# A sink column in the score tile and one triangle select instead of two: a sliding-window attention stage inside a two-layer trunk on one core

## The chip, the core and the metric

The kernel runs on one core of a Trainium2 chip. The time is the device time of one execution in microseconds (us). Before the change, three runs took 959.68, 959.81 and 960.17 us (median 959.81). The execution that the profiler recorded took 959.31 us; its span from the first to the last instruction is 957.6 us.

## The reference

Two layers, each on a sequence of 512 tokens with 1024 channels. One projection of the normalised input gives the columns of two branches: a gated linear recurrence (8 heads of 128) and a sliding-window attention (16 query heads of 64 channels, 2 key/value heads, window 128, a learned sink per head). Both are gated, joined, projected back, normalised and added to the input. The attention part, cut to what matters:

```python
# per block n of 128 queries: keys of block n-1 and of block n
s = einsum('bnqkgd,bnskd->bnkgqs', qb, kw) * ATT_SCALE
band = (diff >= 0) & (diff < WINDOW)          # diff = query position - key position
s = where(mask, s, NEG_INF)
p = softmax(concatenate([s, sink], axis=-1), axis=-1)[..., :-1]
o = einsum('bnkgqs,bnskd->bnqkgd', p, vw)
```

A query at place t of its block sees keys s <= t of its own block and keys s > t of the block before, so exactly 128 keys; the sink only adds to the softmax's sum (and to its maximum).

## The kernel before, in words

All activations stay in SBUF; weights stream from memory in 136 pieces of 128x512 per layer. Each piece is split into two fp32r parts, whi on ScalarE (L169) and wlo = raw - whi on VectorE (L170; a few on GpSimd), and every projection product is three matmuls (L175 to L177).

`step()` issues one such triple and lets the conversions of later pieces run ahead. `merge()` interleaves a branch's own stream with the projection of the slabs that come next. The list ORDER sets the order of slabs: keys and values, queries (QA), recurrence inputs (IV), FQ, and so on. After the last query slab, `run()` merges the attention stream with all the projection up to and including the slab FQ. The order of instructions on each engine is then laid down by the compiler's planner, which follows the order in the program where its own times allow; the matmuls in `pin(...)` keep their order among themselves.

The attention stream has 16 steps a layer: 4 groups g of 4 heads by 4 query blocks n. Step i does three things with projection steps between them:

- `att_scores(g, n)`: for n = 0 eight matmuls into one score tile S; for n > 0 eight matmuls of 256 columns (two heads, key blocks n-1 and n) into two tiles S, one after the other. There are three such PSUM tiles (`sc`), taken in turn, and the transposes use them too. VectorE folds the two key blocks into one (L432: where s > t the score of the block before replaces that of the own block), takes the maximum (L433), and makes the exponent's bias from maximum and sink (L436) and the sink's exponent (L438). ScalarE makes four exponents with their sums (L442) and that of the sink (L445). VectorE adds it (L446) and inverts the sum (L447). GpSimd scales P (L449).
- `att_transpose`, two steps later: TensorE transposes P (L455), ScalarE and VectorE split the result into two fp32r halves (L267, L268, tile tag `a`, 2 buffers). For n > 0 GpSimd's affine_select makes two masked copies of both halves (L467): `pcur`, the keys s <= t for the own block (tags `b` and `oy` in turn), and `pprev`, the keys s > t for the block before (tag `q`, 4 buffers).
- `att_value`, four steps later: matmuls of the masked copies with the values of their blocks (L481; 2 for n = 0, 4 for n > 0), a copy on ScalarE (L483) and two additions on VectorE (L487).

`kv_evac` (L327 to L366) rotates the keys of a token tile and stores the values as `vst`; `kst` holds the transposed keys by block. After the attention, `hgrn` begins with a reciprocal per head into a tile of tag `a` (L551). Query tiles of FQ and the rotation tables use tag `q` too.

Of the kernel before, what the change touches and what calls it, by code (L numbers as in the profile page):

```python
# [10 lines left out]
F32 = mybir.dt.float32  # L11
# [54 lines left out]
def hybrid_kernel(ctx: ExitStack, tc: tile.TileContext, x, wkv, win, wout, g_pre, g_post, lbp, ghead, sinks,  # L66
# [28 lines left out]
    def tmp(tag, dt=F32, n=1):  # L95

        t = tp.tile([P, n, 512] if n > 1 else [P, 512], dt, tag=tag, name=tag, bufs=TB[tag])
        return t
# [225 lines left out]
    def layer(l, last):  # L324
        hops = lambda k, tt: tuple(t[:, k, tt * P:(tt + 1) * P] for t in hT[l])

        kst, vst, rot, oa = [], [], [], []  # L327

        def kv_evac(tt, o):
# [24 lines left out]
            def rest():  # L354
                kt = sc()
                ts_ = slice(tt * P, (tt + 1) * P)
# [49 lines left out]
        def att_scores(g, n):  # L406
# [6 lines left out]
            if n == 0:  # L413
                S = sc()
                for h in range(4):
                    for p in range(2):
                        pin(nc.tensor.matmul(S[:, h * P:(h + 1) * P], lhsT=q[:, h, t_], rhs=kst[v][p][:, 0:P],
# [5 lines left out]
            else:  # L423
                for hp_ in range(2):
                    S = sc()
                    for h in range(2):
                        for p in range(2):
                            pin(nc.tensor.matmul(S[:, h * 256:(h + 1) * 256], lhsT=q[:, 2 * hp_ + h, t_],  # L428
                                             rhs=kst[v][p][:, (n - 1) * P:(n + 1) * P],
                                             start=(h == 0 and p == 0), stop=(h == 1 and p == 1)))  # L430
                    Sv = S.rearrange("p (h s) -> p h s", h=2)
                    nc.vector.copy_predicated(Sv[:, :, P:2 * P], am2, Sv[:, :, 0:P])  # L432
                    nc.vector.tensor_reduce(mx_[:, 2 * hp_:2 * hp_ + 2], Sv[:, :, P:2 * P], axis=AX.X, op=ALU.max)  # L433
                    cur += [Sv[:, h, P:2 * P] for h in range(2)]
            negm = sm.tile([P, 4], F32, tag="negm", name="negm")
            nc.vector.scalar_tensor_tensor(negm, mx_, -SCALE, nsnk[:, l, hs], op0=ALU.mult, op1=ALU.min)  # L436
            ds_ = sm.tile([P, 4], F32, tag="ds", name="ds")
            nc.vector.tensor_tensor(ds_, snk[:, l, hs], negm, op=ALU.add)  # L438
            pt = tmp("s")
            sums = sm.tile([P, 4], F32, tag="sums", name="sums")  # L440
            for h in range(4):
                nc.scalar.activation(pt[:, h * P:(h + 1) * P], cur[h], AF.Exp, bias=negm[:, h:h + 1], scale=SCALE,  # L442
                                     accum_out=sums[:, h:h + 1])
# [4 lines left out]
            pv = pt.rearrange("p (h s) -> p h s", h=4)  # L448
# [3 lines left out]
        def att_transpose(g, n, pt, odd):  # L452
# [3 lines left out]
            tt_ = tmp("a", F32R, 2)  # L456
            split_psum(tt_[:, 0], tt_[:, 1], T)
            if n == 0:
                return [(n, tt_[:, 0]), (n, tt_[:, 1])]
            terms = []  # L460
            for which in range(2):
                if which == 0:
# [446 lines left out]
```

## Time and profile before

| | |
|---|---|
| median of three runs | 959.81 us |
| the profiled execution, its span | 959.31 us, 957.6 us |
| busy: TensorE, VectorE, ScalarE, GpSimd | 921.2, 683.7, 478.4, 268.9 us |
| attention stage of layer 0, of layer 1 (read from the trace) | about 79 to 192 us, 551 to 664 us |
| steps with n > 0 | 12 a layer |

PE stands for TensorE's matmuls, DVE for VectorE, ACT for ScalarE, POOL for GpSimd. Busy times of PE contain the filling of its pipeline. "Idle before" is time in which the engine had nothing to run, with the instruction that ended the wait. A line with x2 or more is several instructions of one kind in a row, with the time from the first's start to the last's end.

### The profile page before, as it was taken

How to read it: one execution, taken by the hardware profiler on the slowest of the kernel's cores; microseconds unless marked ns; L12 is line 12 of the kernel's file. 1: busy time of each engine (PE TensorE's matmuls, PEld its weight loads, DVE VectorE, ACT ScalarE, POOL GpSimd, SP SyncE). 2: the span in 40 equal slices, each digit the busy share in tenths (PEclk: the TensorE clock that was granted, in tenths of full speed). 3: DMA queues.
4: the chain of work that ended last, by engine and by line, in shares of the span. 5: the costliest groups of instructions: out<-in, count | busy, mean ns of one | idle time of the engine just before them, and what ended most of it. 6: DMA issues, size and time to landing. Idle time of an engine off the chain costs nothing.

```text
span 957.6 us, 19092 instructions
## 1 busy us (share of the span) xinstructions
PE 921.2 (96%) x7228; PEld 757.5 (79%) x7228; DVE 683.7 (71%) x1382; ACT 478.4 (50%) x1135; POOL 268.9 (28%) x282
## 2 busy tenths in 40 slices
PE   7999999999999999999979998999999999999996
PEld 5888777777878888788868886877788887887885
DVE  5766888786757785765794678878867568849546
ACT  5434656836545462334552365676374545514242
POOL 2322454422231221211231234434322213113102
PEclk9999999999999999999989999999999999999998
DMA  6366433122413343324452775112223123513313
GB/s 227 101 197 201 137 81 89 52 71 67 122 46 89 90 132 89 107 71 112 133 163 66 198 209 155 34 56 88 79 58 98 55 79 100 155 51 107 88 45 132
DMA packets 56716, 101.34 MB, mean 106 GB/s; under 512 B 6448, under 2 KB 8880, under 8 KB 56624
## 3 DMA queue, kind: packets, MB, share of 16 engines
q1 hardware_dynamic: 56624, 100.12, 35.1%
q8 instruction: 57, 0.93, 0.4%
q14 instruction: 35, 0.29, 0.1%
HBM read 87.52 MB, written 12.58 MB: 105 GB/s over the span
## 4 chain that ended last, share of the span: by engine, by line
PE 78%; DVE 11%; ACT 6%; issue 2%; POOL 2%; DMA 1%; SPq 0%; DVEq 0%; POOLq 0%; ACTq 0%
PE pj L175 22%; PE pj L177 22%; PE pj L176 21%; DVE wlo L170 3%; PE sc L583 2%; PE sc L428 2%; PE ac L652 1%; ACT s L442 1%; PE ac L655 1%; PE ac L640 1%; DVE oa L487 1%; PE ac L481 1%; DVE q L600 1%; PE sc L455 1%; PE sc L700 1%
## 5 line engine op out<-in xcount | busy, mean ns | idle before, releaser
L169 ACT CAST whi<-raw 128x512 fp32r<-128x512 f32 x256 | 157.2, 621 | 131.2 <-PE pj L177 61.0
L170 DVE TENSOR_TENSOR wlo<-raw,whi 128x512 fp32r<-128x512 f32 x248 | 190.1, 778 | 44.8 <-ACT whi L169 42.4
L175 PE MATMUL pj<-hhi,wlo 128*128 128x512 f32 x512 | 206.0, 402 | 0.0
L177 PE MATMUL pj<-hhi,whi 128*128 128x512 f32 x512 | 200.1, 391 | 0.0
L176 PE MATMUL pj<-hlo,whi 128*128 128x512 f32 x512 | 199.5, 390 | 0.0
L177 PEld LDWEIGHTS pj<-hhi,whi 128*128 128x128 f32 x512 | 96.1, 188 | 21.0
L175 PEld LDWEIGHTS pj<-hhi,wlo 128*128 128x128 f32 x512 | 96.2, 188 | 18.6
L176 PEld LDWEIGHTS pj<-hlo,whi 128*128 128x128 f32 x512 | 96.3, 188 | 18.0
L175 PE MATMUL pj<-whi,ops 128*128 128x512 f32 x256 | 103.8, 406 | 0.0
L175 PE MATMUL pj<-whi,hlo 128*128 128x512 f32 x256 | 103.0, 405 | 0.0
L176 PE MATMUL pj<-wlo,hhi 128*128 128x512 f32 x256 | 102.1, 399 | 0.0
L177 PE MATMUL pj<-whi,hhi 128*128 128x512 f32 x256 | 101.4, 396 | 0.0
L177 PE MATMUL pj<-whi,ops 128*128 128x512 f32 x256 | 100.1, 391 | 0.0
L176 PE MATMUL pj<-wlo,ops 128*128 128x512 f32 x256 | 99.7, 390 | 0.0
L601 POOL TENSOR_TENSOR k<-k,tot 128x256 f32<-128x256 f32 x80 | 66.0, 844 | 109.5 <-PE sc L583 60.5
L600 DVE TENSOR_TENSOR q<-q,tot 128x256 f32<-128x256 f32 x80 | 48.3, 629 | 14.5 <-PE sc L594 7.6
L442 ACT ACTIVATE s<-sc,negm 128x128 f32<-128x128 f32 x128 | 45.6, 370 | 25.7 <-DVE negm L436 25.4
L449 POOL TENSOR_TENSOR s<-s,sums 128x512 f32<-128x512 f32 x32 | 34.4, 1074 | 83.4 <-DVE sums L447 47.9
L177 PEld LDWEIGHTS pj<-whi,hhi 128*128 128x128 f32 x256 | 48.9, 191 | 10.2
L177 PEld LDWEIGHTS pj<-whi,ops 128*128 128x128 f32 x256 | 48.0, 188 | 10.7
L176 PEld LDWEIGHTS pj<-wlo,hhi 128*128 128x128 f32 x256 | 49.2, 192 | 8.4
L175 PEld LDWEIGHTS pj<-whi,hlo 128*128 128x128 f32 x256 | 48.8, 191 | 8.6
(172 smaller groups left out, 1594.8 us busy)
## 6 DMA issues: line engine op xcount, KB each, us to landing
raw<-in_win_dram SPq DMA_DIRECT2D x192, 256.0 KB, 2.7
raw<-in_wout_dram SPq DMA_DIRECT2D x64, 256.0 KB, 2.7
stack<-rot SPq DMA_DIRECT2D x16, 512.0 KB, 4.4
qs<-stack SPq DMA_DIRECT2D x32, 256.0 KB, 5.0
a<-in_x_dram SPq DMA_DIRECT2D x12, 256.0 KB, 2.9
raw<-in_wkv_dram SPq DMA_DIRECT2D x8, 256.0 KB, 4.0
x_mid<-a SPq DMA_DIRECT2D x8, 256.0 KB, 2.1
a<-x_mid SPq DMA_DIRECT2D x8, 256.0 KB, 2.9
```

The lines of the kernel that those rows point to most:

```text
L169: nc.scalar.copy(hi, v)
L170: (nc.gpsimd if i in on_pool and i % 2 else nc.vector).tensor_tensor(lo, v, hi.bitcast(F32), op=ALU.subtract)
L175: nc.tensor.matmul(o, lhsT=sta[1], rhs=mov[0], start=start, stop=False)
L176: nc.tensor.matmul(o, lhsT=sta[0], rhs=mov[1], start=False, stop=False)
L177: nc.tensor.matmul(o, lhsT=sta[0], rhs=mov[0], start=False, stop=stop)
L428: pin(nc.tensor.matmul(S[:, h * 256:(h + 1) * 256], lhsT=q[:, 2 * hp_ + h, t_], rhs=kst[v][p][:, (n - 1) * P:(n + 1) * P], start=(h == 0 a ...
L442: nc.scalar.activation(pt[:, h * P:(h + 1) * P], cur[h], AF.Exp, bias=negm[:, h:h + 1], scale=SCALE, accum_out=sums[:, h:h + 1])
L449: nc.gpsimd.tensor_tensor(pv, pv, sums.unsqueeze(2).broadcast_to([P, 4, P]), op=ALU.mult)
L455: pin(nc.tensor.transpose(T[:, h * P:(h + 1) * P], pt[:, h * P:(h + 1) * P], ident))
L583: pin(nc.tensor.matmul(L[32 * b:32 * b + 32, c:c + 16], lhsT=k[:, o_:o_ + 32], rhs=qv[:, blk:blk + qu, 1, :], start=True, stop=True, tile_ ...
L600: nc.vector.tensor_tensor(qv[:, :, 1, :], qv[:, :, 1, :], tv[:, :, 0].unsqueeze(2).broadcast_to([P, nb, hh]), op=ALU.mult)
L601: nc.gpsimd.tensor_tensor(kv_[:, :, 0, :], kv_[:, :, 0, :], tv[:, :, 1].unsqueeze(2).broadcast_to([P, nb, hh]), op=ALU.mult)
```

## The change: what it does

For n > 0 the sink becomes one more column of the score tile. The key blocks are stored in falling order (`kst`), so that S holds the own block in columns 0 to 127 and the block before in columns 128 to 255. Key 0 of the block before is never seen; its column 128 is overwritten by the sink divided by the scale (a two-element copy on ScalarE for each S, from the new constant `snk8`). The fold now replaces own columns 1 to 127 where s > t, the maximum and the exponents run over 129 columns, and the sum comes out with the sink in it. The separate sink exponent, its input and its addition remain for n = 0 alone, and the bias becomes a plain multiplication.

For the values, P transposed (both halves, now in a tile of tag `q` for all steps) goes whole to the values of the block before, and one select (s <= t) goes to a stationary of differences, v of the own block minus v of the block before (`vdf`, one buffer of tag `a`, three subtractions with splits a layer in `kv_evac`). Counts of matmuls stay as they are.

```diff
+            kvs[tt] = raw
+            if tt == 1:
+                vdf.append(tmp("a", F32R, 2).rearrange("p v (n c) -> p v n c", n=NT))
+            if tt:
+                dv = sm.tile([P, 2, 64], F32, tag="dv", name="dv", bufs=1)
+                two = lambda r: r[:, 128:256].rearrange("p (v d) -> p v d", v=2)
+                nc.vector.tensor_tensor(dv, two(raw), two(kvs.pop(tt - 1)), op=ALU.subtract)
+                nc.scalar.copy(vdf[0][:, :, tt, 0:64], dv)
+                nc.vector.tensor_tensor(vdf[0][:, :, tt, 64:128], dv, vdf[0][:, :, tt, 0:64].bitcast(F32), op=ALU.subtract)
...
-                    nc.vector.copy_predicated(Sv[:, :, P:2 * P], am2, Sv[:, :, 0:P])
-                    nc.vector.tensor_reduce(mx_[:, 2 * hp_:2 * hp_ + 2], Sv[:, :, P:2 * P], axis=AX.X, op=ALU.max)
-                    cur += [Sv[:, h, P:2 * P] for h in range(2)]
+                    nc.scalar.copy(Sv[:, :, P:P + 1], snk8[:, l, 4 * g + 2 * hp_:4 * g + 2 * hp_ + 2].unsqueeze(2))
+                    nc.vector.copy_predicated(Sv[:, :, 1:P], am2[:, :, 1:P], Sv[:, :, P + 1:2 * P])
+                    nc.vector.tensor_reduce(mx_[:, 2 * hp_:2 * hp_ + 2], Sv[:, :, 0:P + 1], axis=AX.X, op=ALU.max)
+                    cur += [Sv[:, h, 0:P + 1] for h in range(2)]
...
-            nc.vector.scalar_tensor_tensor(negm, mx_, -SCALE, nsnk[:, l, hs], op0=ALU.mult, op1=ALU.min)
-            ds_ = sm.tile([P, 4], F32, tag="ds", name="ds")
-            nc.vector.tensor_tensor(ds_, snk[:, l, hs], negm, op=ALU.add)
-            pt = tmp("s")
+            if n:
+                nc.vector.tensor_scalar(negm, mx_, -SCALE, None, op0=ALU.mult)
...
-            es = sm.tile([P, 4], F32, tag="es", name="es")
-            nc.scalar.activation(es, ds_, AF.Exp)
-            nc.vector.tensor_tensor(sums, sums, es, op=ALU.add)
+            if n == 0:
...
-            tt_ = tmp("a", F32R, 2)
+            tt_ = big.tile([P, 2, 512], F32R, tag="q", name="pall", bufs=QB)
...
-            for which in range(2):
...
+            d = big.tile([P, 2, 512], F32R, tag="oy", name="pcur", bufs=6) if odd else tmp("b", F32R, 2)
+            nc.gpsimd.affine_select(out=d.rearrange("p a (h t) -> p (a h) t", h=4),
...
+            whole, own = terms
+            prods = [(vst[v][:, max(n - 1, 0), :], whole[:, j]) for j in range(2)]
+            if own is not None:
+                prods += [(vdf[0][:, v, n, :], own[:, j]) for j in range(2)]
...
+    snk8 = const.tile([P, DEPTH, ATT_HEADS], F32, name="snk8")
+    nc.vector.tensor_scalar(snk8, snk, 1.0 / SCALE, None, op0=ALU.mult)
```

## Rows read from the trace of the kernel before

**Rows 1.** The page: busy time, share and instructions of each engine; the chain that ended last, by engine.
```profile
PE 921.2 (96%) x7228; PEld 757.5 (79%) x7228; DVE 683.7 (71%) x1382; ACT 478.4 (50%) x1135; POOL 268.9 (28%) x282
...
PE 78%; DVE 11%; ACT 6%; issue 2%; POOL 2%; DMA 1%; SPq 0%; DVEq 0%; POOLq 0%; ACTq 0%
```

**Rows 2.** Busy time of each engine in the attention stages of layer 0 and of layer 1. Columns: stretch, its length, busy us (and instructions) of PE, PE's weight loads, DVE, ACT, POOL, granted clock as a share, DMA share, GB/s.
```profile
79.00:192.00 113.00, 106.26 (x534) 87.08 (x533) 89.01 (x201) 74.79 (x228) 50.09 (x44) 0.97 0.37 108
...
551.00:664.00 113.00, 106.08 (x540) 86.81 (x539) 91.00 (x202) 76.42 (x229) 50.06 (x44) 0.98 0.39 108
```

**Rows 3.** The timeline of PE: the instructions before which it sat idle longest in the two attention stages, and one in layer 1's key/value stage (start us, duration, instruction, idle before it and what ended it).
```profile
105.33 0.84 PE L455 MATMUL sc<-ident,s 128*128 128x128 f32 x4 [1.96 <-DVE negm L436]
...
125.44 1.40 PE L417 MATMUL sc<-kst,qs 128*128 128x128 f32 x8 [1.73 <-ACT s L442]
...
154.69 0.74 PE L428 MATMUL sc<-kst,qs 128*128 128x256 f32 x4 [0.36 <-ACT s L442]
...
161.51 1.43 PE L428 MATMUL sc<-kst,qs 128*128 128x256 f32 x8 [1.27 <-ACT s L442]
...
185.06 0.73 PE L481 MATMUL ac<-pcur,vst 128*128 128x512 f32 x2 [0.56 <-POOL pcur L467]
186.55 0.73 PE L481 MATMUL ac<-pprev,vst 128*128 128x512 f32 x2 [0.30 <-POOL pprev L467]
...
500.99 0.39 PE L175 MATMUL pj<-wkv,hlo 128*128 128x256 f32 x1 [0.94 <-DVE hlo L268]
...
577.90 0.63 PE L455 MATMUL sc<-ident,s 128*128 128x128 f32 x4 [1.95 <-DVE negm L436]
```

**Rows 4.** The timeline of POOL and of DVE ahead of the first three of those gaps.
```profile
98.03 1.10 POOL L467 TENSOR_SCALAR_AFFINE_SELECT pcur<-a 128x1024 fp32r<-128x1024 f32 x1 [0.24 <-DVE negm L436]
99.08 1.54 POOL L467 TENSOR_SCALAR_AFFINE_SELECT pprev<-a 128x1024 fp32r<-128x1024 f32 x1
...
98.21 2.96 DVE L170 TENSOR_TENSOR wlo<-raw,whi 128x512 fp32r<-128x512 f32 x2 [0.18 <-ACT whi L169]
101.09 0.15 DVE L438 TENSOR_TENSOR ds<-snk,negm 128x4 f32<-128x4 f32 x1
...
102.03 0.69 DVE L170 TENSOR_TENSOR wlo<-raw,whi 128x512 fp32r<-128x512 f32 x1
...
119.89 3.92 DVE L170 TENSOR_TENSOR wlo<-raw,whi 128x512 fp32r<-128x512 f32 x3
...
121.73 1.54 POOL L467 TENSOR_SCALAR_AFFINE_SELECT pprev<-a 128x1024 fp32r<-128x1024 f32 x1
...
154.49 1.55 POOL L467 TENSOR_SCALAR_AFFINE_SELECT pprev<-a 128x1024 fp32r<-128x1024 f32 x1
...
153.61 1.47 DVE L170 TENSOR_TENSOR wlo<-raw,whi 128x512 fp32r<-128x512 f32 x1 [0.24 <-ACT whi L169]
155.00 1.04 DVE L446 TENSOR_TENSOR sums<-sums,es 128x4 f32<-128x4 f32 x1
```

**Rows 5.** Groups of instructions by line in layer 0's attention stage (79 to 192 us): count, busy us and mean ns of one, idle time before them and what ended it.
```profile
L170 DVE TENSOR_TENSOR wlo<-raw,whi 128x512 fp32r<-128x512 f32 x25 | 24.4, 994 | 2.3 <-ACT whi L169 1.7
...
L467 POOL TENSOR_SCALAR_AFFINE_SELECT pprev<-a 128x1024 fp32r<-128x1024 f32 x12 | 15.8, 1320 | 0.0
...
L446 DVE TENSOR_TENSOR sums<-sums,es 128x4 f32<-128x4 f32 x16 | 5.1, 318 | 8.2 <-ACT es L445 8.1
...
L445 ACT ACTIVATE es<-ds 128x4 f32<-128x4 f32 x16 | 3.4, 215 | 0.5 <-DVE ds L438 0.5
```

**Rows 6.** Busy time by short stretches around the first gaps (columns as in rows 2; the granted clock is the third number from the end).
```profile
104.00:112.00 8.00, 6.67 (x29) 5.59 (x29) 6.00 (x15) 3.23 (x15) 5.71 (x6) 0.79 0.27 102
120.00:128.00 8.00, 6.27 (x31) 5.21 (x30) 6.64 (x13) 3.59 (x13) 4.31 (x4) 0.88 0.88 228
128.00:136.00 8.00, 8.00 (x39) 6.48 (x38) 6.63 (x15) 4.92 (x20) 5.32 (x5) 0.91 0.01 2
592.00:600.00 8.00, 6.27 (x29) 5.23 (x28) 6.60 (x14) 3.35 (x12) 3.66 (x3) 0.82 0.82 201
```

**Rows 7.** The timeline of one step with n > 0, from its score matmuls to the next step's: PE, DVE, and the first and the last of ACT's four exponents.
```profile
129.59 0.64 PE L428 MATMUL sc<-kst,qs 128*128 128x256 f32 x4
...
132.54 0.43 DVE L432 COPY_PREDICATED sc<-masks,sc 128x256 f32<-128x256 uint8 x1 [0.47 <-PE sc L428]
...
133.93 0.82 DVE L436 SCALAR_TENSOR_TENSOR negm<-mx,nsnk 128x4 f32<-128x4 f32 x1
...
134.83 0.37 ACT L442 ACTIVATE s<-sc,negm 128x128 f32<-128x128 f32 x1
...
135.88 0.37 ACT L442 ACTIVATE s<-sc,negm 128x128 f32<-128x128 f32 x1
...
135.69 0.74 PE L428 MATMUL sc<-kst,qs 128*128 128x256 f32 x4
```

**Rows 8.** A group of the whole span that stands near what the change adds (columns as in rows 5).
```profile
L268 DVE TENSOR_TENSOR kst<-sc,kst 128x128 fp32r<-128x128 f32 x16 | 4.5, 280 | 0.0
```

**Rows 9.** The timeline of DVE in layer 1's key/value stage and at the beginning of layer 0's recurrence, and the busy times of 8 us near the end of layer 0's attention stage (columns as in rows 2).
```profile
502.55 0.68 DVE L170 TENSOR_TENSOR wlo<-raw,whi 128x512 fp32r<-128x512 f32 x1
...
192.18 1.74 DVE L551 RECIPROCAL a<-f 128x256 f32<-128x256 f32 x1
...
168.00:176.00 8.00, 8.00 (x44) 6.72 (x43) 4.04 (x12) 7.89 (x19) 1.72 (x2) 1.00 0.00 0
```

More of the change, by code (lines that the diff above doesn't have):

```diff
@@ L95, in tmp @@
     def tmp(tag, dt=F32, n=1):
-        t = tp.tile([P, n, 512] if n > 1 else [P, 512], dt, tag=tag, name=tag, bufs=TB[tag])
+        t = tp.tile([P, n, 512] if n > 1 else [P, 513] if tag == "s" else [P, 512], dt, tag=tag, name=tag, bufs=TB[tag])
+        t = t[:, 0:512] if tag == "s" else t
         return t
@@ L325, in layer @@
         hops = lambda k, tt: tuple(t[:, k, tt * P:(tt + 1) * P] for t in hT[l])
-        kst, vst, rot, oa = [], [], [], []
+        kst, vst, vdf, rot, oa, kvs = [], [], [], [], [], {}
         def kv_evac(tt, o):
@@ L416, in att_scores @@
                     for p in range(2):
-                        pin(nc.tensor.matmul(S[:, h * P:(h + 1) * P], lhsT=q[:, h, t_], rhs=kst[v][p][:, 0:P],
+                        pin(nc.tensor.matmul(S[:, h * P:(h + 1) * P], lhsT=q[:, h, t_], rhs=kst[v][p][:, (NT - 1) * P:NT * P],
                                          start=(h == 0 and p == 0), stop=(h == 3 and p == 1)))
@@ L440, in att_scores @@
+            pt = tp.tile([P, 513], F32, tag="s", name="pt", bufs=TB["s"])
             sums = sm.tile([P, 4], F32, tag="sums", name="sums")
             for h in range(4):
-                nc.scalar.activation(pt[:, h * P:(h + 1) * P], cur[h], AF.Exp, bias=negm[:, h:h + 1], scale=SCALE,
+                nc.scalar.activation(pt[:, h * P:(h + 1) * P + (n > 0)], cur[h], AF.Exp, bias=negm[:, h:h + 1], scale=SCALE,
                                      accum_out=sums[:, h:h + 1])
-            es = sm.tile([P, 4], F32, tag="es", name="es")
@@ L445, in att_scores @@
-            nc.scalar.activation(es, ds_, AF.Exp)
-            nc.vector.tensor_tensor(sums, sums, es, op=ALU.add)
+            if n == 0:
+                ds_, es = (sm.tile([P, 4], F32, tag=t, name=t) for t in ("ds", "es"))
+                nc.vector.tensor_tensor(ds_, snk[:, l, hs], negm, op=ALU.add)
+                nc.scalar.activation(es, ds_, AF.Exp)
+                nc.vector.tensor_tensor(sums, sums, es, op=ALU.add)
             nc.vector.reciprocal(sums, sums)
-            pv = pt.rearrange("p (h s) -> p h s", h=4)
+            pv = pt[:, 0:512].rearrange("p (h s) -> p h s", h=4)
@@ L455, in att_transpose @@
                 pin(nc.tensor.transpose(T[:, h * P:(h + 1) * P], pt[:, h * P:(h + 1) * P], ident))
[L456 removed]
+            tt_ = big.tile([P, 2, 512], F32R, tag="q", name="pall", bufs=QB)
             split_psum(tt_[:, 0], tt_[:, 1], T)
             if n == 0:
[L459 to L472 removed]
+                return tt_, None
+            d = big.tile([P, 2, 512], F32R, tag="oy", name="pcur", bufs=6) if odd else tmp("b", F32R, 2)
+            nc.gpsimd.affine_select(out=d.rearrange("p a (h t) -> p (a h) t", h=4),
+                                    in_=tt_.bitcast(F32).rearrange("p a (h t) -> p (a h) t", h=4),
+                                    pattern=[[0, 8], [1, P]], compare_op=ALU.is_ge, fill=0.0, base=0, channel_multiplier=-1)
+            return tt_, d
         def att_value(g, n, terms):
@@ L479, in att_value @@
             U = ac()
-            for i, (blk, d) in enumerate(terms):
-                pin(nc.tensor.matmul(U, lhsT=vst[v][:, blk, :], rhs=d, start=(i == 0), stop=(i == len(terms) - 1)))
+            whole, own = terms
+            prods = [(vst[v][:, max(n - 1, 0), :], whole[:, j]) for j in range(2)]
+            if own is not None:
+                prods += [(vdf[0][:, v, n, :], own[:, j]) for j in range(2)]
+            for i, (sta, mov) in enumerate(prods):
+                pin(nc.tensor.matmul(U, lhsT=sta, rhs=mov, start=(i == 0), stop=(i == len(prods) - 1)))
             ul = tmp("u")
```

16 lines of the change are left out of this document (4 added, 12 removed).

## The prediction

> **What bounds the kernel now.** I read the page's busy times and its chain first. PE is busy for 921.2 of 957.6 us, and 78% of the chain that ended last is PE [rows 1]. The change leaves PE's instructions as they are: for n > 0 eight score matmuls of 256 columns, four transposes, four value matmuls, before and after. So it can only win or lose where PE waits, or runs at half its clock.
>
> The second view is the busy time by stage. In the two attention stages PE is idle for 113.00 - 106.26 = 6.7 us and 113.00 - 106.08 = 6.9 us; DVE is busy for 89 and 91 of 113 us, ACT for 75 and 76, POOL for 50 and 50 [rows 2]. No engine but PE is full there, so the question is which wait ends last.
>
> The third is PE's own timeline. Few gaps hold nearly all of that idle time: in layer 0 1.96, 1.73, 0.36 and 1.27 us, where the transposes or scores wait for a PSUM tile that the bias or the exponents of an earlier step still hold, and 0.56 and 0.30 us at the end, where the last value product waits for the two selects [rows 3]. Layer 1 repeats this (its first, 1.95 us, is shown). I take 5.3 us a layer for the first four and 0.86 for the last two.
>
> What made the exponents late? The timeline of DVE and POOL ahead of the gaps shows it: two conversions wlo took 2.96 us together and three took 3.92, while one alone takes 0.69; beside them POOL ran pcur and pprev, which themselves took up to 1.55 us instead of 1.10 [rows 4]. The mean wlo of the stage is 994 ns [rows 5]. A 4-element addition took 1.04 us beside a select [rows 4], its mean being 318 [rows 5]. DVE and POOL hold each other up, the bias of the next step queues behind wlo on DVE, and PE runs dry.
>
> The Trainium skill ("SBUF — State Buffer", section "Who interferes with whom") gives the rule: DVE and POOL share a port pair that one instruction holds to its end, and a DVE instruction contends with a reading GpSimd one if both its inputs lie in SBUF. By it the bias of a step with n > 0, a multiplication with one tensor input after the change, would no longer be held up (it took 0.82 us once); no row here separates the two forms of it, and the sum below doesn't count on it.
>
> Last the clock: it is 0.79 of full in 104 to 112 us, 0.88 and 0.91 in 120 to 136, 0.82 in 592 to 600 [rows 6], each behind a gap of 1.7 us or more; the chip's levels being 2.4 and 1.2 GHz, these are means over stretches at half speed. The time given away is 8 x (0.21 + 0.12 + 0.09 + 0.18) = 4.8 us.
>
> **The change, part by part.**
>
> *Select.* 24 selects go (12 pprev a layer, 15.8 us of POOL busy time in layer 0 [rows 5]). At each gap I take away what the second select cost. Gap 1: 2.96 - 2 x 0.69 = 1.58 us were lost beside selects of 1.10 and 1.54 us; the second's share by length is 0.92, and as the first still delays the pair I take 0.8. Gap 2: 3.92 - 3 x 0.69 = 1.85, half of it 0.9. Gaps 3 and 4: the addition that took 1.04 us disappears, and half of 1.47 - 0.69, 0.4; 1.4 together. The sink's two additions on DVE go as well, some 0.15 us each when nothing holds them up [rows 4]; they stand in the same queue: 0.3 at gaps 1 and 2, 0.2 at gap 4. That is 1.1 + 1.2 + 1.6 = 3.9 of 5.3 us a layer. The bounds: 0, if DVE only waits elsewhere instead, and all 5.3.
>
> *Sink column.* 48 small ACT copies come (two a step), 24 sink exponents of 215 ns go [rows 5]. A 2-element copy isn't in the trace; the nearest row is that exponent, so I take 0.2 us. What matters is the place: the copy has to wait for the S matmuls, and the fold, being written after it and in the same tile, then waits for ACT's queue. Behind the fold on DVE stand the maximum, the bias, and the next wlo; PE waits for these. Before, the fold waited for PE alone [rows 7]. If ACT is free the link costs 0.2; if it has just begun four exponents, 135.88 + 0.37 - 134.83 = 1.4 us and the last reading of the sum more [rows 7], 1.6 in all. ACT is two thirds busy, but much of that can be ordered around the copy, so I take 0.2 + 0.25 for each of the three gaps: 1.35 us a layer against the 3.9, leaving 2.55. From below: nothing, where DVE has other work. From above: 2 x 1.8 at each, which eats the gain twice over.
>
> *Tail.* The products with the whole transposed P need no select, and one select less stands ahead of the last: the second gap goes, the first stays, 0.3 us a layer (0 to 0.86). Against it, ACT is busy for 7.89 of 8 us at 168 to 176 [rows 9]; three steps there bring six copies for three exponents, 6 x 0.2 - 3 x 0.215 = 0.6 us, of which I charge half, 0.3.
>
> *Value differences.* Three times a layer DVE does two operations of 128 columns (the nearest row is 280 ns [rows 8]) and ACT one: 1.7 us of DVE a layer. They are written behind the keys of token tile 1 and later, so behind the last half of the normalised input that PE waits for at 500.99 us [rows 3]. The wlo at 502.55 [rows 9] stands behind the first of them; I charge 0.3 a layer (0 to 0.6). Without that cover it is 1.7 a layer.
>
> *Constant snk8.* One small DVE operation at the start: 0.15 us alone, 1.04 held up by POOL [rows 4]. I take 0.2, nearest to the first.
>
> *Buffers.* `pall` takes one of four `q` tiles for all 16 steps and lives until its value product two steps on: three are live, and one more when the first query tile of FQ comes, where the next split waits for a product that PE did a step before. I charge nothing (0 to 0.5). `vdf` holds one of two `a` tiles until the last value product at 186.55 + 0.73 us; the second reciprocal starts at 192.18 [rows 9], so nothing.
>
> *Clock.* With gaps of about 1.1 us instead of 1.7 to 2.0, the falls should mostly go: the gap of 1.27 us had none behind it, though the one of 1.95 in layer 1 had none either. I take 60% of 4.8: 2.9 (0 to 4.8).
>
> *Sum:* 2 x (2.55 + 0.3) + 2.9 = 8.6 saved; 2 x (0.3 + 0.3) + 0.2 = 1.4 paid; 7.2 us net. The profiled execution took 959.31, so 952.1; the median lies 0.5 above it: 952.6 us.
>
> **Rivals.** About 0.2% (1.9 us) is what a measurement of this kernel can tell from no change.
>
> *All gaps go.* If one select never meets two wlo in a row and the copies fall into ACT's free time, 2 x 6.2 + 4.8 us go and 1.4 are paid: 944. For it: DVE gets rid of some 12 x 0.63 us of small work a layer besides. Against it: the scaling of P, a further POOL operation of 1 us per step, still meets wlo, and all orders change. Chance 0.12.
>
> *The link gives back what the select gave.* The fold waits for ACT about as long as DVE waited for POOL; gaps move, the clock falls as often: 959.8, within 1.9. For it: DVE already waits 8.1 us a layer for ACT's sink exponent [rows 5], and would now wait for two copies a step in its place. Chance 0.17.
>
> *Slower: the link becomes the limit.* In the step shown, S was computed at 129.59 and the next S in the same tile started at 135.69, right when the exponents freed it [rows 7]: 6.1 us of chain in a step of 113 / 16 = 7.06. If each of the two folds waits 1.2 us for ACT, 2.4 are added and perhaps 0.67 (the bias at 0.15, like other small operations, instead of 0.82) saved: the chain is 7.8 us, 0.8 above the step. It decides from 0.95 + 0.67 = 1.6 us a step on. Half of the 24 steps so hit cost 9 us, and the old gaps that remain are paid back by the selects, some 2 to 3: 966. For it: ACT's queue is in order, and copies that the planner puts behind four exponents wait that long. Against: most steps have PE work between to cover it. Chance 0.25.
>
> The Trainium skill ("PSUM — Partial Sum Buffer", section "PSUM bank collisions raise a hardware error") speaks for this rival: two engines must be kept apart by bank, not by address, so the fold has to wait for the copy though their columns differ. No row of before has ACT writing PSUM beside DVE.
>
> My forecast has 0.46. Its own range, from the bounds of the link and of the clock, is 948 to 957. Over all cases I give 944 to 964. Faster by over 0.2%: 0.46 + 0.12 + 0.01 of the second rival = 0.59; same 0.16; slower 0.25.
>
> **What would show it.** Right: POOL's busy time in the stage near 35 us instead of 50; the mean wlo well under 994 ns; PE idle for some 4 us a layer in the stage instead of 6.8; at most one stretch under full clock there; the sink copies at about 0.2 us with short waits of the fold for them. The link is wrong if the fold's waits for ACT sum to over 20 us a layer and PE's gaps end at exponents. The differences are wrong if PE's gap in the key/value stage grows beyond 0.94 + 0.6. The prediction as a whole falls if wlo becomes short and PE's gaps stay: then it wasn't POOL that starved PE.

## The result, and the profile after

The changed kernel took 963.73 us (median of 9 runs, 959.54 to 965.32), the kernel before 959.94 us beside it (9 runs): a ratio of 1.0027, 95% interval 1.0015 to 1.0040. It is slower by 0.27%, where a gain of 7.2 us was forecast. The execution that the profiler recorded took 964.37 us. The nine executions fall into two bunches, three at 959.5 to 960.7 us and six at 963.5 to 965.3; e9 below bears on that.

The page of the changed kernel, the lines that answer to [rows 1]:

```profile
PE 924.9 (96%) x7228; PEld 756.1 (79%) x7228; DVE 667.8 (69%) x1347; ACT 494.8 (51%) x1171; POOL 241.0 (25%) x258
...
PE 66%; DVE 9%; ACT 8%; issue 5%; POOL 2%; DMA 1%; DVEq 0%; POOLq 0%; ACTq 0%
```

DVE and POOL lost work (16 and 28 us), ACT gained 16 us. The first score product comes at 82.90 us instead of 79.18, so the two attention stages are read 4 us later than in [rows 2]; the columns are the same:

```profile
83.00:196.00 113.00, 106.36 (x535) 84.68 (x534) 79.69 (x172) 80.60 (x239) 34.46 (x30) 0.99 0.42 115
555.00:668.00 113.00, 106.83 (x535) 85.21 (x534) 77.82 (x170) 80.65 (x239) 34.39 (x30) 0.98 0.40 113
```

POOL fell from 50 to 34.4 us and the clock rose from 0.97 to 0.99 in layer 0, yet PE still idles 6.6 us there. Where, its timeline says (idle before in brackets, as in [rows 3]):

```profile
95.01 0.96 PE L176 MATMUL pj<-whi,hlo 128*128 128x512 f32 x3 [1.19 <-ACT whi L170]
...
108.22 1.11 PE L427 MATMUL sc<-kst,qs 128*128 128x128 f32 x8 [0.61 <-ACT pt L456]
...
182.99 0.70 PE L494 MATMUL ac<-pall,vst 128*128 128x512 f32 x2 [0.49 <-DVE oa L500]
...
192.93 0.66 PE L471 MATMUL sc<-ident,pt 128*128 128x128 f32 x4 [2.15 <-POOL pt L465]
...
567.68 0.98 PE L176 MATMUL pj<-whi,hlo 128*128 128x512 f32 x3 [1.66 <-ACT whi L170]
```

The gaps of 1.96, 1.73 and 1.27 us are gone. In their place stand two of another kind: a projection that waits for a weight conversion on ACT (95.01; 567.68 is its twin in layer 1), and at the end 2.15 us before the transposes of the last P. The clock falls behind that last one in layer 0 and behind the first one in layer 1; another fall is at the start of the kernel:

```profile
32.00:40.00 8.00, 8.00 (x36) 6.92 (x37) 7.51 (x33) 5.41 (x19) 2.65 (x2) 0.79 0.49 131
...
192.00:200.00 8.00, 7.07 (x26) 5.73 (x27) 7.85 (x13) 5.81 (x11) 3.50 (x4) 0.79 0.25 66
...
568.00:576.00 8.00, 7.54 (x36) 6.10 (x35) 4.68 (x10) 3.96 (x15) 0.52 (x1) 0.79 0.72 243
```

Taking the first score product and the recurrence's first product as milestones: 3.7 us were lost before the first score product (82.90 against 79.18), 0.4 in layer 0's attention (123.70 against 123.34 us, though at the better clock), 1.4 in layer 1's (123.51 against 122.14).

**What made the last P late.** ACT's timeline in the last two steps of layer 0's attention, and POOL's ahead of the last transposes; of ACT only exponents (x1 each) and table loads are copied, of the last step the first and the last exponent:

```profile
166.28 0.38 ACT L456 ACTIVATE pt<-sc,negm 128x129 f32<-128x129 f32 x1
...
166.77 0.37 ACT L456 ACTIVATE pt<-sc,negm 128x129 f32<-128x129 f32 x1
...
167.25 1.28 ACT L539 ACT_TABLE_LOAD   x1
...
169.16 1.28 ACT L456 ACT_TABLE_LOAD   x1
170.45 0.37 ACT L456 ACTIVATE pt<-sc,negm 128x129 f32<-128x129 f32 x1
...
170.93 1.28 ACT L540 ACT_TABLE_LOAD   x1
...
172.84 1.28 ACT L456 ACT_TABLE_LOAD   x1
174.14 0.37 ACT L456 ACTIVATE pt<-sc,negm 128x129 f32<-128x129 f32 x1
...
184.07 0.37 ACT L456 ACTIVATE pt<-sc,negm 128x129 f32<-128x129 f32 x1
...
189.19 0.38 ACT L456 ACTIVATE pt<-sc,negm 128x129 f32<-128x129 f32 x1
...
190.16 1.28 POOL L478 TENSOR_SCALAR_AFFINE_SELECT b<-pall 128x1024 fp32r<-128x1024 f32 x1 [8.69 <-DVE pall L269]
191.41 1.47 POOL L465 TENSOR_TENSOR pt<-pt,sums 128x512 f32<-128x512 f32 x1
```

The last step but one spreads its four exponents over 8.2 us, the last one over 5.5 (184.07 to 189.19 + 0.38), with weight conversions and a gate's activation between them. Before, four lasted 1.4 us, as in [rows 7] (134.83 to 135.88 + 0.37). The scaling of the last P then stood behind a select on POOL that had begun 0.02 us before the inverted sum was there, and PE waited 2.15 us; in layer 1, where the exponents took 4.4 us, it waited 0.98. In the 8.2 us the gates' activations (L539, L540) stand between the exponents, and as these need another function table, each change costs a load of 1.28 us: 28 loads in the span, 22 before. What holds the exponents apart shows in the compiled order of ACT, which names the semaphores that each instruction waits for (Activation_49 is ACT's own):

```
L456 ACTIVATE pt,sums<-sc_79,negm 128x128 [waits DVE_49,PE_49]
L456 ACTIVATE pt,sums<-sc_79,negm 128x128 x3
...
L456 ACTIVATE pt,sums<-sc_80,negm 128x129 [waits DVE_49,Activation_49]
L456 ACTIVATE pt,sums<-sc_80,negm 128x129 [waits Activation_49]
L456 ACTIVATE pt,sums<-sc_78,negm 128x129 [waits Activation_49] x2
```

The heads stand 128 columns apart in `pt`, but an exponent now writes 129. Its last column is the next head's first, so the next exponent must wait until this one's write is done: ACT waits for itself. The 128-column exponents of n = 0 wait for nothing between them.

**And the link**, the fold's wait for the sink copy on ACT. The first step with n > 0 (PE, ACT, DVE, and ACT again: the first exponent and the conversions behind the fourth):

```profile
85.19 1.12 PE L438 MATMUL sc<-kst,qs 128*128 128x256 f32 x8
...
88.97 0.37 ACT L456 ACTIVATE pt<-sc,negm 128x128 f32<-128x128 f32 x1 [2.41 <-DVE negm L451]
...
90.46 0.26 ACT L443 COPY sc<-snk 128x2 f32<-128x2 f32 x2
...
90.69 0.42 DVE L444 COPY_PREDICATED sc<-masks,sc 128x254 f32<-128x254 uint8 x1
...
92.52 0.37 ACT L456 ACTIVATE pt<-sc,negm 128x129 f32<-128x129 f32 x1 [1.80 <-DVE negm L449]
...
94.35 1.65 ACT L170 CAST whi<-raw 128x512 fp32r<-128x512 f32 x3
```

The scores are there at 86.31 us. The copies stand behind the step before's exponents in ACT's queue, and the fold behind the copies: 4.4 us. (Not all of this is the link: in e6 below, without it, the fold of this step still starts 2.6 us after the scores.) The bias and the exponents follow, ACT idling 1.80 us, and behind the exponents the weight conversions for which PE then waits (95.01 above). Over a layer's 24 score tiles the mean from the end of the score product to the start of its fold, worked out from the timelines, is 1.50 us against 0.87 before.

The groups of the stage (79 to 195 us) show the same from the other side:

```profile
L171 DVE TENSOR_TENSOR wlo<-raw,whi 128x512 fp32r<-128x512 f32 x29 | 24.4, 856 | 9.4 <-ACT whi L170 9.1
...
L444 DVE COPY_PREDICATED sc<-masks,sc 128x254 f32<-128x254 uint8 x24 | 9.8, 418 | 2.3 <-ACT sc L443 2.1
...
L443 ACT COPY sc<-snk 128x2 f32<-128x2 f32 x24 | 3.8, 165 | 5.2 <-PE sc L438 5.2
...
L463 DVE RECIPROCAL sums<-sums 128x4 f32<-128x4 f32 x16 | 2.8, 176 | 14.8 <-ACT pt L456 11.0 <-ACT sc L443 3.7
```

DVE's mean wlo fell from 994 ns to 856, a copy takes 165 ns. But DVE now idles for ACT: 9.1 us at wlo, 14.7 at the reciprocal, 2.1 at the fold, where it was 1.7 at wlo and 8.1 at the sum before [rows 5]. Which of these waits cost anything, the experiments have to tell.

### The profile page after: what moved, and what is told of

Same layout as the page of the kernel before. It is cut to its first block, busy times and chain, and to the rows that moved or that the text cites. A ratio compares the mean times of both kernels' runs of the same rounds, so it can differ in the third digit from the quotient of the medians.

```text
span 962.6 us, 19077 instructions
## 1 busy us (share of the span) xinstructions
PE 924.9 (96%) x7228; PEld 756.1 (79%) x7228; DVE 667.8 (69%) x1347; ACT 494.8 (51%) x1171; POOL 241.0 (25%) x258
## 4 chain that ended last, share of the span: by engine, by line
PE 66%; DVE 9%; ACT 8%; issue 5%; POOL 2%; DMA 1%; DVEq 0%; POOLq 0%; ACTq 0%
PE pj L176 18%; PE pj L178 18%; PE pj L177 18%; ACT pt L456 3%; PE sc L596 2%; DVE wlo L171 2%; PE ac L665 1%; PE ac L494 1%; ACT whi L170 1%; PE sc L438 1%; PE ac L668 1%; PE ac L653 1%; PE sc L471 1%; DMA raw<-in_win_dram 1%; POOL pt L465 1%
## 5 line engine op out<-in xcount | busy, mean ns | idle before, releaser
L171 DVE TENSOR_TENSOR wlo<-raw,whi 128x512 fp32r<-128x512 f32 x248 | 184.9, 756 | 51.7 <-ACT whi L170 49.6
L465 POOL TENSOR_TENSOR pt<-pt,sums 128x512 f32<-128x512 f32 x32 | 35.8, 1118 | 109.9 <-DVE sums L463 95.6
L178 PEld LDWEIGHTS pj<-whi,ops 128*128 128x128 f32 x256 | 48.0, 188 | 10.6
L176 PEld LDWEIGHTS pj<-whi,ops 128*128 128x128 f32 x256 | 48.1, 188 | 9.4
```

Of the source, the lines that this page charges most:

```text
L171: (nc.gpsimd if i in on_pool and i % 2 else nc.vector).tensor_tensor(lo, v, hi.bitcast(F32), op=ALU.subtract)
L176: nc.tensor.matmul(o, lhsT=sta[1], rhs=mov[0], start=start, stop=False)
L178: nc.tensor.matmul(o, lhsT=sta[0], rhs=mov[0], start=False, stop=stop)
L465: nc.gpsimd.tensor_tensor(pv, pv, sums.unsqueeze(2).broadcast_to([P, 4, P]), op=ALU.mult)
```

## The experiments

All ratios are against the kernel before on the same chip, with 95% intervals. The main theory: one select less is worth what was forecast, and the sink column takes it back by two separate costs: the exponents put in series because each writes into the next one's place (below, the overlap), and the copy in front of the fold (the link). The rivals are in the texts on record. Four runs came first.

**e1: heads 129 columns apart in P.**

```diff
-            pt = tp.tile([P, 513], F32, tag="s", name="pt", bufs=TB["s"])
+            pt = tp.tile([P, 516], F32, tag="s", name="pt", bufs=TB["s"])
+            W_ = P + (n > 0)
...
-                nc.scalar.activation(pt[:, h * P:(h + 1) * P + (n > 0)], cur[h], AF.Exp, ...
+                nc.scalar.activation(pt[:, h * W_:(h + 1) * W_], cur[h], AF.Exp, ...
```

> The change with one thing altered: the exponents of the four heads are written 129 columns apart instead of 128, so that no head's sink column lies on the next head's first column. Theory A (the overlap makes each exponent wait for the one before, and lets the planner put other work between them): exponents of a step start 0.34 us apart again instead of 0.49, the function-table loads on ACT fall from 28 to 22, the attention stream ends some 10 us earlier than in the changed kernel, PE's waits in the attention stages fall by 3 to 5 us a layer: 955 to 958 us. Theory B (the sink copy in front of the fold is what costs): the time stays within 2 us of the changed kernel's 963.7. Theory C (the loss is all in the start stage): 962 to 964 us.

**e2: the select alone** (the scores, the sink and the order of keys' use as before; the one select and the value differences as changed, with the keys in rising order; diff against the kernel before).

```diff
-            for which in range(2):
...
-                d = big.tile([P, 2, 512], F32R, tag="q", name="pprev", bufs=QB)
...
+            return tt_, d
```

> The kernel before with the select part alone: one select, whole P to the values of the block before, value differences; the sink as it was. Theories A and B: the prediction's term for the selects stands by itself, PE's waits in the attention stages fall by 2 us a layer or more and the clock falls less often: 950 to 956 us. Theory C: the key/value stage of layer 0 costs the same 3 us here, because the value differences cause it: 957 to 961 us.

**e3: without the constant** (the copy scales the sink itself).

```diff
-                    nc.scalar.copy(Sv[:, :, P:P + 1], snk8[...].unsqueeze(2))
+                    nc.scalar.activation(Sv[:, :, P:P + 1], snk[...].unsqueeze(2), AF.Copy, scale=float(1.0 / SCALE))
...
-    nc.vector.tensor_scalar(snk8, snk, 1.0 / SCALE, None, op0=ALU.mult)
```

> The change without its constant snk8: the sink copy multiplies by 8 itself on ACT, one small DVE operation less at the start. Theory C1 (that one operation moves the key rotation of layer 0 behind a DVE operation that GpSimd holds up, 1.94 us of PE idle instead of 0.90, and a fall of the clock behind it): the first score matmul comes at 79 to 81 us instead of 82.9, the time is 960 to 962 us. Rival C2 (the value differences or chance do it): first score matmul at 82 to 83.5, 963 to 965 us.

**e4: the sink column alone** (two selects and the two stationaries of values as before; diff against the changed kernel).

```diff
-            return tt_, d
+            for which in range(2):
...
-                nc.vector.tensor_tensor(dv, two(raw), two(kvs.pop(tt - 1)), op=ALU.subtract)
```

> The kernel before with the sink column alone: 129 columns, sink copies, both selects kept. Theory A: exponents 0.49 us apart, more table loads than before (30 by the order of the program), slower than before by 4 us or more: 964 to 970 us. Theory B: the same time, but with the fold's waits for ACT's copies above 10 us a layer. If neither, it is within 2 us of before.

| | median us | ratio |
|---|---|---|
| e1 | 958.64 | 0.9972 (0.9958 to 0.9986) |
| e2 | 951.13 | 0.9896 (0.9877 to 0.9916) |
| e3 | 961.00 | 1.0004 (0.9990 to 1.0018) |
| e4 | 970.35 | 1.0093 (1.0074 to 1.0113) |

The select alone gives 10 us, the sink column alone costs 9: the sum is 1.1 us under the kernel before, where the changed kernel is 2.6 above it; e9 below finds most of that difference at the start. In e2 the stage shows what the forecast had described, the gaps with their old causes but smaller:

```profile
106.12 0.63 PE L464 MATMUL sc<-ident,s 128*128 128x128 f32 x4 [1.08 <-DVE negm L445]
...
124.07 1.11 PE L426 MATMUL sc<-kst,qs 128*128 128x128 f32 x8 [0.92 <-ACT s L451]
```

They were 1.96 and 1.73 us [rows 3], and no stretch of the stage is under full clock:

```profile
80.00:193.00 113.00, 108.59 (x556) 88.35 (x555) 90.85 (x212) 76.57 (x232) 35.45 (x32) 1.00 0.41 115
```

In e1 the table loads are back at 22 and a block of four exponents at 1.55 us (3.1 in the changed kernel), while the time from scores to fold stays at 1.48: the two costs come apart. The time is 0.6 us above e1's range, and one sign failed: PE's waits were to fall by 3 to 5 us a layer, and fell from 6.6 to 6.0 and from 6.2 to 5.8; the gap at the weight conversion stays (1.15 us in layer 0). e4 ends 0.35 us above its range. e3 is not apart from the kernel before, nor clearly from the changed one; its time lies in the theory's range, but its first score product still comes at 82.61 us, as the rival had it. The constant isn't needed for the late start.

Then the two costs were taken one at a time.

**e5: the sink copy on DVE** (pitch 129).

```diff
-                    nc.scalar.copy(Sv[:, :, P:P + 1], snk8[...].unsqueeze(2))
+                    nc.vector.tensor_copy(Sv[:, :, P:P + 1], snk8[...].unsqueeze(2))
```

> The changed kernel with a pitch of 129 columns a head in pt (as in the run e1, 958.6 us) and the sink copy moved from ScalarE to VectorE, right in front of its fold. Nothing of the computation is changed. Theory 'two costs' (serialised exponents, which the pitch has taken away, and the link through ScalarE): the fold no longer waits for ScalarE, so the time from the last score product to the fold's start falls from 1.5 us towards the 0.9 us of the kernel before; the copy itself stands on VectorE with about 0.17 to 0.25 us, 48 times in a layer's 24 steps, 8 to 12 us a layer of VectorE's time that mostly lies beside other work. I expect 952 to 956 us and the sum of the gaps of TensorE in the two attention stages down from 6 to under 5.5 us a layer. Rival 'any op in front of the fold costs the same, whichever engine holds it': 957 to 960 us, gaps at 6 us. Rival 'VectorE becomes the limit': 960 us and more, with gaps that end at folds whose own wait is VectorE's queue.

**e6: the copy behind the maximum** (pitch 129; fold and maximum over 128 columns, the bias by the minimum with the sink).

```diff
-                    nc.scalar.copy(Sv[:, :, P:P + 1], snk8[...].unsqueeze(2))
...
-                    nc.vector.tensor_reduce(mx_[:, 2 * hp_:2 * hp_ + 2], Sv[:, :, 0:P + 1], axis=AX.X, op=ALU.max)
+                    nc.vector.tensor_reduce(mx_[:, 2 * hp_:2 * hp_ + 2], Sv[:, :, 0:P], axis=AX.X, op=ALU.max)
+                    nc.scalar.copy(Sv[:, :, P:P + 1], snk8[...].unsqueeze(2))
...
+            nc.vector.scalar_tensor_tensor(negm, mx_, -SCALE, nsnk[:, l, hs], op0=ALU.mult, op1=ALU.min)
```

> The changed kernel with a pitch of 129 columns in pt, but fold and maximum run over the 128 key columns alone, ScalarE's sink copy comes behind the maximum, and the bias takes the sink in by the minimum with nsnk as in the kernel before. The exponent still covers 129 columns, so the small ops for the sink's exponent and its addition stay away. The computation is whole. Theory 'link': nothing stands between the score products and the fold any more, the copy waits on ScalarE in front of the exponents that follow it on the same engine anyway: 950 to 954 us, beside the 951.1 us of the select alone (e2), with the time from score products to the fold at 0.9 to 1.0 us. Rival 'the copies themselves cost (48 ScalarE ops a layer, between exponents)': 955 to 959 us.

**e7: the overlap alone** (diff against the changed kernel; maximum and bias as in e6).

```diff
-                    nc.scalar.copy(Sv[:, :, P:P + 1], snk8[...].unsqueeze(2))
...
-            if n == 0:
+            if True:
                 ds_, es = (sm.tile([P, 4], F32, tag=t, name=t) for t in ("ds", "es"))
```

> The one select with value differences (e2, 951.1 us), the keys in the reversed order, and exponents over 129 columns at a pitch of 128, so that each writes one column of the next head's place; no sink copy, the sink is added by the four small ops of the kernel before. Column 128 holds the score of a key outside the window, so the row sums take in one extra score. Theory 'serialised exponents': each exponent starts only once the one before has ended, 0.49 us apart instead of 0.34, other work of ScalarE gets between them, with up to six more table loads of 1.28 us a layer; the block of four lasts about 3 us instead of 1.55, and the time is 954 to 958 us. Rival 'the overlap costs nothing by itself, it was the copy': 951 to 952 us.

**e8: e7 with heads 129 columns apart** (the diff of e1 on top).

> The same as e7 with a pitch of 129 columns a head, so that no two exponents write one column; the extra score stays in the sums. Theory 'serialised exponents': the block of four exponents is back at about 1.55 us, the order on ScalarE that of e2, and the time 950.5 to 952.5 us; the difference from e7 is the price of the overlap alone. Rival 'one column more for each exponent, or the reversed keys, cost': as e7.

| | median us | ratio |
|---|---|---|
| e5 | 954.50 | 0.9934 (0.9917 to 0.9951) |
| e6 | 951.31 | 0.9900 (0.9884 to 0.9915) |
| e7 | 958.01 | 0.9976 (0.9964 to 0.9988) |
| e8 | 950.32 | 0.9899 (0.9883 to 0.9915) |

e7 and e8 differ in nothing but the distance of the heads, and by 0.0077 of 960 us: 7.4 us (each lies within 0.2 us of its range). ACT's exponents in the first step with n > 0, in e7 (its second and third):

```profile
91.10 0.37 ACT L452 ACTIVATE pt<-sc,negm 128x129 f32<-128x129 f32 x1
91.37 0.19 ACT L452 ACTIVATION_READ_ACCUMULATOR pt<-sc,negm 128x1 f32 x1
91.59 0.37 ACT L452 ACTIVATE pt<-sc,negm 128x129 f32<-128x129 f32 x1
```

and in e8:

```profile
88.14 0.37 ACT L453 ACTIVATE pt<-sc,negm 128x129 f32<-128x129 f32 x1 [0.36 <-DVE negm L447]
88.40 0.19 ACT L453 ACTIVATION_READ_ACCUMULATOR pt<-sc,negm 128x1 f32 x1
88.50 0.36 ACT L453 ACTIVATE pt<-sc,negm 128x129 f32<-128x129 f32 x1
...
88.84 0.37 ACT L453 ACTIVATE pt<-sc,negm 128x129 f32<-128x129 f32 x1
```

Each takes 0.37 us in both; they start 0.49 us apart in e7, 0.36 and 0.34 in e8. The 0.14 us make 3 x 0.14 us in 24 steps, 10 us of ACT time, part of it beside other work. More is what gets in between: a block of four lasts 2.79 us in the mean against 1.55, with 26 table loads against 22. How the price divides between the two wasn't measured.

e6 leaves nothing of the copy's cost that the medians show (0.9900 against e2's 0.9896). Its first step with n > 0:

```profile
85.29 1.12 PE L438 MATMUL sc<-kst,qs 128*128 128x256 f32 x8
...
88.96 0.75 DVE L443 COPY_PREDICATED sc<-masks,sc 128x254 f32<-128x254 uint8 x2
...
90.42 0.27 ACT L445 COPY sc<-snk 128x2 f32<-128x2 f32 x2
...
90.91 0.37 ACT L454 ACTIVATE pt<-sc,negm 128x129 f32<-128x129 f32 x1 [0.22 <-DVE negm L448]
...
92.30 1.67 ACT L170 CAST whi<-raw 128x512 fp32r<-128x512 f32 x3
...
93.76 0.84 PE L176 MATMUL pj<-whi,hlo 128*128 128x512 f32 x3
```

The copies stand where they stood, at the end of ACT's exponents; the folds now run 1.5 us ahead of them, behind DVE's own earlier work alone. The mean from scores to fold is 0.69 us. This step's scores were there 0.1 us later than in the changed kernel, its exponents begin 1.6 us earlier and the weight conversions behind them 2.05, and the projection at 93.76 doesn't wait, where in the changed kernel PE idled 1.19 us before it and 0.48 behind it. That is how the link reached PE. In both layers together PE idles 6.8 us in e6's stages against 11.9 in e1's.

e5 is half a miss: the time fell as expected, but the fold still starts 1.30 us after the scores, where I had looked for 0.9, and from the end of a step's first scores to the end of its last exponent it takes 8.7 us, longer than e1's 7.0. It is faster than e1 all the same, and PE's gap at the weight conversion is gone in it: from a layer's first score product to the first conversion behind the exponents it takes 9.6 us in e5 (79.61 to 89.24), 11.4 in e1 (80.59 to 91.98). Whether that is all of the difference isn't shown. (The texts of e5 and e6 count 48 copies a layer; there are 24, 48 in both.)

The last four runs: one for the start, two for the sum of the costs, and the change without any of them.

**e9: the gate constants later.** The changed kernel's start, DVE, POOL and PE, is where most of the 3.7 us were lost:

```profile
30.12 0.16 DVE L862 TENSOR_SCALAR lb_a<-lb 128x16 f32<-128x16 f32 x1
30.20 1.24 DVE L864 TENSOR_SCALAR lb_b<-lb 128x16 f32<-128x16 f32 x1
31.35 0.21 DVE L352 TENSOR_TENSOR s<-km 128x64 f32<-128x64 f32 x1
...
30.13 1.28 POOL L171 TENSOR_TENSOR wlo<-raw,whi 128x512 fp32r<-128x512 f32 x1 [3.32 <-ACT whi L170]
...
31.95 0.44 PE L359 MATMUL sc<-ident,s 128*128 128x128 f32 x2 [1.94 <-ACT s L353]
```

lb_a took 0.16 us; lb_b, of the same kind and size, began 0.07 us behind a POOL wlo and took 1.24, and the key op behind it was late. PE's gap is 1.94 us (0.90 before), and behind it the clock is 0.79.

```diff
             until(lambda: 0 in qs)
+            lb_consts()
...
-    nc.vector.tensor_scalar(lb_b, lb, FLOOR, None, op0=ALU.max)
```

> The changed kernel with one thing moved: the eleven small VectorE ops that make the gate constants (lb_den to lb_c), which stand between the first tile's key ops at the start, are emitted behind the first query tile, where their readers are still far off. Nothing else is changed. Theory 'a toss at the start': in the changed kernel's profile the op lb_b starts 0.07 us behind a GpSimd wlo, is held 1.24 us by it, and the key op behind it and the first key transposes are late (TensorE's gap 1.94 us, then a stretch under full clock); without these ops the key op is done 0.8 us earlier and clear of that wlo, so every run is like the good ones (959.5 to 960.7 us): I expect a median of 959 to 961 us and the stretch from the first key and value product to the first score product at 64.5 to 65.5 us instead of 67.8. Rival 'the spread of 959.5 to 965.3 us is from elsewhere': 963 to 964 us as before.

**e10: the copy late, the overlap left in** (e6's diff without e1's).

> The changed kernel with the copy of the sink behind the maximum (as e6), but the exponents at a pitch of 128 columns as the change has them, so that each overlaps the next head's place. The computation is whole. With the changed kernel (963.7 us: copy in front, overlap), e1 (958.6: copy in front, no overlap) and e6 (951.3: copy late, no overlap) this fills a square. Theory 'two costs that add up': 951.3 us and the 7.7 us between e7 and e8: 957 to 960 us, the block of four exponents at about 2.8 us. Rival 'the overlap costs only where the copy is in front of the fold': 951 to 954 us.

**e11: the sink column alone, heads 129 columns apart** (e4 with e1's diff).

> The sink column alone on the kernel before (two selects of the transposed P and no value differences, as e4), with the exponents at a pitch of 129 columns. Theory 'two costs that add up': e4's 970.35 us less the 5.1 to 7.7 us that the overlap costs, 962.5 to 965.5 us; what is left over the kernel before, 2 to 5 us, is the link through ScalarE. Rival 'with GpSimd's two selects as the limit the overlap is hidden': 968 us and more.

**e12: e6 with the gate constants later.**

> The late copy with the pitch of 129 columns (e6) and the gate constants moved as in e9: all the costs found taken out of the change, the computation whole. Theory: e6's runs without its late start (949.8 to 951.4 us), so 949 to 950.8 us, and a first-score stretch of 64.5 to 65.5 us. Rival 'the start was not lost in e6's other runs': 951.3 us.

| | median us | ratio |
|---|---|---|
| e9 | 959.79 | 0.9997 (0.9984 to 1.0010) |
| e10 | 957.18 | 0.9958 (0.9942 to 0.9974) |
| e11 | 964.98 | 1.0039 (1.0022 to 1.0056) |
| e12 | 949.14 | 0.9882 (0.9860 to 0.9905) |

The square of the two costs, as ratios:

| | heads 128 apart | 129 apart |
|---|---|---|
| copy in front of the fold | 1.0027 (the change) | 0.9972 (e1) |
| copy behind the maximum | 0.9958 (e10) | 0.9900 (e6) |

The overlap costs 0.0055 and 0.0058 (5.3 and 5.6 us), the copy's place 0.0069 and 0.0072 (6.6 and 6.9 us). But these differences hold the start too: it was late in the profiles of the change, e6 and e10, in time in e1's. The stretch from a layer's first score product to the recurrence's first product leaves it out, and holds the same 638 instructions of PE in every run. Both layers' stretches added, worked out from the timelines, in us (before: 245.5; e2: 236.5):

| | heads 128 apart | 129 apart |
|---|---|---|
| copy in front of the fold | 247.2 (the change), 245.3 (e9, the same attention) | 242.9 (e1) |
| copy behind the maximum | 240.3 (e10) | 234.7 (e6) |

Here the overlap costs 2.4 to 4.3 us with the copy in front, 5.6 with it behind and 7.1 without a copy (e7 243.1, e8 236.0); the copy's place costs 4.9 to 6.9 and 8.2; both together 10.5 to 12.5. The medians of e9 and e12, with the constants moved in both, lie 0.0115 apart: 11.0 us. So each costs time by itself, and both some 11 us; that they simply add up isn't shown, the overlap cost less beside the other. e11 against e4 gives 0.0054 by the medians and 9.0 us by the stretch (254.6 to 245.6), e11's start being late. What e11 has left over the kernel before, 3.7 us, isn't the link, as its text had it: its stretch is that of the kernel before (245.6, 245.5), and its way to the first score product is 3.4 us longer. e12 is the best, 11.3 us under the kernel before.

In e9 the last key op is over before POOL's wlo begins:

```profile
29.00 0.21 DVE L352 TENSOR_TENSOR s<-km 128x64 f32<-128x64 f32 x1
...
30.14 1.30 POOL L171 TENSOR_TENSOR wlo<-raw,whi 128x512 fp32r<-128x512 f32 x1 [3.90 <-ACT whi L170]
```

The way from the first key and value product to the first score product fell from 67.8 to 64.7 us, and the time by 0.0030 (2.9 us), to e9's single bunch of 958.7 to 962.5 us; from e6 to e12 it is 0.0018 (1.7 us). Without e9's move the key op falls on either side of POOL's wlo: it was late in the profiles of the changed kernel, e3, e6, e7, e10 and e11, in time in e1, e2, e4, e5 and e8, some with the constant and the value differences and some without. So it is a toss of some 0.1 us in when the conversion starts; the sink column isn't needed for it (e7 has no sink copy and no constant). How often it falls badly in the kernel before (in time in its profile) wasn't tried with the constants moved.

## Why the prediction was wrong

**Select: right in sum.** e2 keeps the sink's two additions, 0.8 us a layer of the 3.9, so the forecast's terms for it are 2 x (3.9 - 0.8 + 0.3) + 2.9 less 2 x 0.3 for the value differences: 9.1, and e2 gives 10. POOL near 35 us (34.4), a shorter wlo, full clock in the stage (e2: 1.00): all seen. That the sum fits so well is in part luck: PE's idle time fell by 2.3 us a layer (in layer 0 from 6.7 to 4.4), where 3.4 were counted, and the clock, priced at 2.9, gave back all it had taken in the two stages, 3.4 and 1.7. The sink's two additions, 1.6 us as priced, don't show in the medians (e6, without them, 0.9900, e2 0.9896); in the stretch of the attention e6 is 1.8 us shorter.

**Sink column: the step that failed.** It was priced at "0.2 + 0.25 for each of the three gaps: 1.35 us a layer", 2.7 in all; its two parts cost some 11 us together (e9 against e12). Two errors. The first is the link's path, and with it its size: 4.9 to 8.2 us. The copy itself was right (165 ns against 0.2), but the link was charged at three gaps only, by way of DVE's maximum, bias and next wlo. It delays the 24 folds of a layer by 0.6 us in the mean, and with them the bias, the exponents and, behind these in ACT's queue, the weight conversions: there PE waited, 1.19 and 1.66 us in the two layers, in layer 1 with a fall of the clock behind it, and with the copy out of the way (e6) it didn't. The sign to look for was wrong too: the forecast named waits of the fold for ACT of over 20 us, yet they sum to 2.1. DVE's long wait at the reciprocal (14.7 us) is no sign of the link either: e6, without the link, has 10.2 there, and the kernel before waits 8.1 at the addition in front of it. The second is an omission: the text priced the exponents' 129th column at nothing and never asked where it is written. That overlap cost 2.4 to 7.1 us, by what stood beside it.

**Rivals.** The time lies between the second (959.8) and the third (966), and the sign is the third's. It also lies inside the 944 to 964 given over all cases, at the very edge, which says nothing for the forecast's mechanism. The third rival's mechanism, the link alone, doesn't reach: with the overlap gone (e1) the link gives back 7 of the select's 10 us and leaves 2.7 us of gain. The Trainium skill ("PSUM — Partial Sum Buffer", section "PSUM bank collisions raise a hardware error") had spoken for it: the fold does wait for the copy of another column (90.69 behind 90.46); whether that is by bank or by the tile no run tells apart.

**Clock: right for the select, wrong in the sum.** In the two attention stages 3.4 and 1.7 us were given away before (summed over short windows), 1.7 and 1.7 after, behind the gaps of 2.15 and 1.66 us, and 1.7 more at the start: nothing of the 2.9 was saved.

**Value differences and constant.** No more than charged: from layer 1's first key and value product to its first score product the changed kernel took 65.69 us against 65.96, and e3 shows nothing for the constant. **The start** was not in the forecast at all, about 2 to 3 us.

**Tail.** The gaps at the last value products, which waited for selects, went; the 2.15 us came from the last step's own exponents under the overlap and from a select in front of its scaling.

## What to carry to other kernels

When an instruction's output grows by a column, look at whose place that column is: here exponents that wrote into one place were put in series, and the planner put work between them, some of which needed another function table; with the place free (e8) it didn't. An instruction of another engine in front of the first reader of a result can cost more than its own length, because it waits its turn in that engine's queue (165 ns, and a fold 0.6 us later in the mean); put it behind the last step that can do without it, and follow the delay to everything that stands behind the late work, not only to the waits known from before. Price an edit in the parts that can be built apart: here one half was worth 10 us and the other cost 11.

## What was not expected of the hardware

Each exponent with a row sum is followed on ACT by a reading of that sum (ACTIVATION_READ_ACCUMULATOR, 0.19 us in the rows of e7 and e8). In e8 the next exponent begins 0.09 us before that reading ends (88.40 + 0.19 against 88.50); in e7, where it waits for ACT's own semaphore, 0.03 us after (91.37 + 0.19 against 91.59). So exponents that write into one place start 0.49 us apart instead of 0.35.

A DVE instruction of 128x16 that takes 0.16 us took 1.24 when it began 0.07 us behind a POOL subtraction of 1.28: it waited for all of it. It has one input, and so has the bias of the changed kernel's steps with n > 0, which takes 0.16 us when nothing holds it up and in e1 once took 1.05, beside a select, and ended with it:

```profile
145.73 1.05 DVE L449 TENSOR_SCALAR negm<-mx 128x4 f32<-128x4 f32 x1
...
145.29 1.48 POOL L479 TENSOR_SCALAR_AFFINE_SELECT pcur<-pall 128x1024 fp32r<-128x1024 f32 x1 [2.55 <-DVE pall L269]
```

The Trainium skill ("SBUF — State Buffer", section "Who interferes with whom") says that such an instruction doesn't contend unless it is in a two-port mode, which it allows for this operation. The forecast took only the first half, for the bias, though its sum didn't count on it; the traces agree with the second: a plain multiplication or maximum with one input can be held.
